# Hybrid attention and retention trunk: a listed first supertile, tables on GpSimd, and outputs loaded two tiles ahead

## The chip, the cores and the metric

The kernel runs on one core of a Trainium2 chip. The time is that of the core on the device, in microseconds (us), from the launch of the program to its end; a profiled execution also gives a span, from the first to the last instruction that the profiler recorded. Engines are named as the profile names them: PE is TensorE, DVE is VectorE, ACT is ScalarE, POOL is GpSimd, SP is SyncE, whose queue issues nearly all DMAs here. Each engine takes its instructions in the order in which they stand in its queue; a waiting instruction holds up all that stand behind it.

## The reference

Two layers and a last RMS norm, on one sequence of 2048 tokens of width 1024:

```
for layer in range(2):
    h    = rms_norm(x, norm_gain[layer])
    proj = h @ w_in[layer]                      # 1024 x 4096: aq ak av ag rq rk rv rg, 512 each
    ya   = chunked attention(aq, ak, av) + relative bias    # 8 heads x 64, own chunk + 8 before
    yr   = retention(rotary(rq), rotary(rk), rv)             # 4 heads x 128, decaying state
    y    = concat(ya * silu(ag), yr * silu(rg))
    x    = x + y @ w_out[layer]                 # 1024 x 1024
out = rms_norm(x, final_gain)
```

The rotary phases come from the positions: cos and sin of position times 64 frequencies. The angles reach 2048 radians, so they are first reduced to (-pi, pi) in several exact steps.

## The kernel before

**Tiles.** The 2048 tokens are 16 tiles of 128, or four supertiles of 512 (n = 0 to 3). The heads are taken in four groups s (two attention heads and one retention head each). For each layer l and each s, the kernel goes through the four supertiles: `dense_T` computes q, k, rq, rk with channels on partitions, `dense_V` computes v, gates and rv with tokens on partitions, and `attention` (which carries `retention` along) works on the supertile whose projections came just before. Every matrix product is made of three float16 products (high with high, high with low, low with high), so one supertile's `dense_T` or `dense_V` is 96 matmuls of 512 columns (L630, L650).

**The normed input.** `norm` makes hT(l, n), the transposed high and low halves of the normed tokens, tile by tile: a sum of squares on ACT (L207), the inverse root on POOL (L210), the product with it on ACT (L231) or DVE (L229), the product with the norm gain, spread to all partitions by a DMA (`gain_load`), on POOL (L233) or DVE, the split on ACT and DVE (L249, L250), and the transposes by DMA (L254, L255) or, for the first four tiles, by PE (`transpose_split`). The four supertiles' hT lie in the pool `hp`, four buffers for each half.

**The tables.** `tables` computes cos and sin of one supertile: 21 short instructions on DVE on 128x256 tiles, two Sin on ACT, and eight DMAs to DRAM (L130 to L133), from where `dense_T` loads them for each s (L559, L560); POOL then turns rq and rk (L595 to L597).

**The order.** PE, ACT, DVE and POOL run in the order in which the Python code emits instructions (`manual_schedule`); the DMAs on SP are ordered by a scheduler. Each generator yields at points about 8 matmuls apart. `run` steps one main generator (dense or output), at each yield also one step of the attention generator, and pulls steps of background work out of the list `bg` (`push(generator, steps)`), spread over the given number of yields (`thirds`). If a table is needed that isn't there, `tab_load` pulls background work until it is. For the first supertile the order is written out by hand (L1005 to L1050), as calls of `go_on` on generators.

**The output stage.** `wout` goes through the 16 tiles. A tile is 48 matmuls (L892) in six steps of eight, two column halves c, each half followed by the residual sum on DVE (L895). Its input is y (written by the attention to DRAM), loaded (`y_load`, L792), measured and scaled by a power of two (`y_scale`, L800 to L811: a sum of squares on ACT for the first six tiles of layer 0 and all of layer 1, else a maximum on DVE, then a product on ACT), split in two float16 rows (`y_split`) and transposed by DMA (`y_turn`). In tile t the step i = 1 splits y of t + 1, i = 2 turns it and loads y of t + 2, i = 5 scales y of t + 2. In layer 0 the sum goes to DRAM (L901) and is normed in place for the next layer (`norm`, one step of it at i = 1, 2, 3, 5, and its transposes at the next tile's i = 0); in layer 1 `final` norms it and stores it. The y tiles, the x tiles (`x_load`, L797) and the weight sections share the four buffers of the pool `w4`.

Of the kernel before, what the change touches and what calls it, by code (L numbers as in the profile page):

```python
# [18 lines left out]
P = 128  # L19
# [8 lines left out]
def hybrid_trunk(ctx: ExitStack, tc: tile.TileContext, x, pos, gain, gcol, w_in, w_out, rel, fgain,  # L28
# [53 lines left out]
    def tables(ns, wks):  # L82

        for n, wk in zip(ns, wks):
            ang, k, r, k2 = (wk[:, i, :] for i in range(4))
            pi = k2.bitcast(I32)
            for hf in range(2):
                o = n * 512 + hf * 256
                sp.dma_start(pi[hf * 64:(hf + 1) * 64, :], pos[None, o:o + 256].to_broadcast([64, 256]))

            def mulsub(dst, kk, c):
                dve.scalar_tensor_tensor(out=dst, in0=kk, scalar=-c, in1=dst, op0=ALU.mult, op1=ALU.add)

            def rnd(dst, src, mul):
                dve.tensor_scalar(dst, src, mul, MAGIC, op0=ALU.mult, op1=ALU.add)
                dve.tensor_scalar(dst, dst, -MAGIC, None, op0=ALU.add)

            dve.tensor_copy(ang, pi)
            dve.tensor_scalar(ang, ang, invf_sb[:, 0:1], None, op0=ALU.mult)
            rnd(k, ang, 1.0 / P1)  # L100
            for c in (PA, PB, PC):
                mulsub(ang, k, c)
            yield
            dve.tensor_scalar(k2, k, -(PD + PE_), None, op0=ALU.mult)
            dve.tensor_tensor(k2, k2, ang, op=ALU.add)
            rnd(k2, k2, 1.0 / TWO_PI)
            mulsub(ang, k2, QA)
            mulsub(ang, k, PD)
            yield
            mulsub(ang, k2, QB)  # L110
            mulsub(ang, k, PE_)
            mulsub(ang, k2, QC)
            yield
            dve.tensor_scalar(ang, ang, PI_CL, -PI_CL, op0=ALU.min, op1=ALU.max)
            dve.tensor_scalar(k, ang, HALF_PI, -TWO_PI, op0=ALU.is_gt, op1=ALU.mult)
            dve.tensor_tensor(k, k, ang, op=ALU.add)
            dve.tensor_scalar(k, k, HALF_PI, PI_CL, op0=ALU.add, op1=ALU.min)
            yield
        for wk in wks:
            ang, k, r, k2 = (wk[:, i, :] for i in range(4))  # L120
            act.activation(r, ang, AF.Sin)
            act.activation(k2, k, AF.Sin)
            dve.tensor_scalar(ang, r, -1.0, None, op0=ALU.mult)
        yield
        for n, wk in zip(ns, wks):
            ang, k, r, k2 = (wk[:, i, :] for i in range(4))
            for hf in range(2):
                sl = slice(hf * 64, hf * 64 + 64)
                cs = slice(hf * 256, hf * 256 + 256)
                sp.dma_start(tab_d[n][0, 0:64, cs], k2[sl, :])  # L130
                sp.dma_start(tab_d[n][0, 64:128, cs], k2[sl, :])
                sp.dma_start(tab_d[n][1, 0:64, cs], ang[sl, :])
                sp.dma_start(tab_d[n][1, 64:128, cs], r[sl, :])  # L133
            tab_done.add(n)
            yield
# [64 lines left out]
    def rms(xt, m, e, nm, junk, on_dve=False):  # L200

        ss = b2.tile([P, 1], F32, tag="ss", name=f"ss{nm}")
        if on_dve:
            dve.tensor_tensor_reduce(out=junk, in0=xt, in1=xt, scale=1.0, scalar=0.0, op0=ALU.mult, op1=ALU.add,
                                     accum_out=ss)
        else:
            act.activation(junk, xt, AF.Square, accum_out=ss)  # L207
        dve.tensor_scalar(ss, ss, m, e, op0=ALU.mult, op1=ALU.add)
        rs = b2.tile([P, 1], F32, tag="rs", name=f"rs{nm}")
        pool.tensor_tensor(rs, ss, mhalf, op=ALU.pow)  # L210
        return rs
# [7 lines left out]
    def norm(l, t, xt, sq_dve=False, mul_dve=False, by_pe=False, rows=None):  # L219
# [5 lines left out]
        rs = rms(xt if sq_dve else xt.rearrange("p (k c) -> p k c", c=P), gains[l].m, gains[l].e, nm,  # L225
                 psS.tile([P, D], F32, tag="S", name=f"pj{nm}") if sq_dve else hh, sq_dve)
# [8 lines left out]
        if by_pe:  # L235
            transpose_split(xt, hh, hl, nm)
            yield
            return
# [5 lines left out]
    def split_rows(xt, nm, rows=None):  # L244
# [4 lines left out]
        act.activation(rows[0], xt, AF.Copy)  # L249
        dve.tensor_tensor(rows[1], xt, rows[0], op=ALU.subtract)  # L250
# [6 lines left out]
    def transpose_split(src, dh, dl, nm):  # L257
        for h in range(2):
            k0, k1 = h * KT // 2, (h + 1) * KT // 2
            pt = psR.tile([P, KT // 2, P], F32, tag="small", name=f"pt{nm}_{h}")  # L260
            for kt in range(k0, k1):
                pe.transpose(pt[:, kt - k0, :], src[:, kt * P:(kt + 1) * P], ident)
            act.activation(dh[:, k0:k1, :], pt, AF.Copy)
            dve.tensor_tensor(dl[:, k0:k1, :], pt, dh[:, k0:k1, :], op=ALU.subtract)
# [108 lines left out]
    def prep_V(l, s, g, quick=False):  # L373
# [16 lines left out]
        def rest(k):  # L390
            for _ in range(0 if quick else k):
                yield
# [793 lines left out]
```

## Time and profile before

| | us |
|---|---|
| median of 3 runs | 2241.95 |
| lowest and highest run | 2240.34 and 2249.49 |
| the profiled execution | 2245.32 |
| its span | 2243.5 |
| PE busy in the span | 2061.8 (92%) |
| DVE, ACT, POOL busy | 1052.2, 1049.1, 813.3 |

The profile is of one execution, which took 3.4 us more than the median; what lies outside its span is 1.8 us. Busy time is the time in which an engine had an instruction under way; PE's matmuls are pipelined, so a matmul's own duration (some 0.38 us) is longer than the step from one to the next (0.22 us).

### The profile page before, as it was taken

The page shows a single profiled execution, that of the slowest core. Times are in us where ns is not written, and L with a number is a line of the kernel's source. Part 1 is how long each engine was busy: PE and PEld are TensorE (multiplying, and loading weights), DVE is VectorE, ACT ScalarE, POOL GpSimd, SP SyncE. Part 2 cuts the span into 40 slices and gives each one's busy share as a digit, 9 for nine tenths or more (in the row PEclk, how much of TensorE's full clock was granted, in tenths as well). Part 3 has the DMA queues.
Part 4 walks back from the last instruction along what each step waited for, and adds up shares of the span by engine and source line. Part 5 has one row for each costly group of instructions (what it writes and reads, how often), then busy time and mean ns, then how long its engine had stood idle before and what let it go on. Part 6 is the DMA issues. An engine that isn't in the chain of part 4 may idle for free.

```text
span 2243.5 us, 37852 instructions
## 1 busy us (share of the span) xinstructions
PE 2061.8 (92%) x13590; PEld 1107.4 (49%) x13590; DVE 1052.2 (47%) x3326; ACT 1049.1 (47%) x1938; POOL 813.3 (36%) x856
## 2 busy tenths in 40 slices
PE   5575999999999999988788999999999999998887
PEld 4233555555555555543333555555555555554333
DVE  5355554445544543456533534454444454445443
ACT  5346454645444544555442545454544454454332
POOL 1444344344443433332223334443454343332100
PEclk9798999999999999999999999999999999999999
DMA  7867555756444644679884445556555455447765
GB/s 212 191 154 166 118 116 123 171 110 133 117 108 103 131 114 90 135 179 235 195 185 127 108 99 111 128 137 146 113 123 118 101 128 121 92 103 170 174 165 145
DMA packets 624541, 308.30 MB, mean 137 GB/s; under 512 B 438080, under 2 KB 580928, under 8 KB 624352
## 3 DMA queue, kind: packets, MB, share of 16 engines
q1 hardware_dynamic: 624352, 305.88, 59.9%
q8 instruction: 107, 1.75, 0.3%
q14 instruction: 82, 0.67, 0.1%
HBM read 123.26 MB, written 41.98 MB: 74 GB/s over the span
## 4 chain that ended last, share of the span: by engine, by line
PE 67%; DMA 7%; ACT 6%; DVE 5%; issue 4%; SPq 2%; POOL 2%; POOLq 0%; ACTq 0%; DVEq 0%
PE dT L630 25%; PE dV L650 25%; PE dO L892 4%; DMA x_d<-xxy 2%; PE S L692 2%; PE S L691 2%; DMA yyy<-y_d 2%; PE o L713 1%; PE o L712 1%; PE o L711 1%; PE r L751 1%; PE r L760 1%; PE r L764 1%; PE r L762 1%; ACT yjy L803 1%
## 5 line engine op out<-in xcount | busy, mean ns | idle before, releaser
L701 POOL TENSOR_TENSOR pq<-sc,pq 128x640 f16<-128x640 f32 (+4 forms) x256 | 320.1, 1250 | 831.9 <-ACT pq L700 423.8
L698 ACT ACTIVATE sc<-sc,mq,cT 128x640 f32<-128x640 f32 (+4 forms) x256 | 218.5, 853 | 646.5 <-DVE mq L697 337.0
L630 PE MATMUL dT<-hTh,whT 128*128 128x512 f16 x1008 | 386.4, 383 | 30.2 <-DMA hTh<-rhn 25.7
L650 PE MATMUL dV<-whV,hTh 128*128 128x512 f16 x1024 | 389.1, 380 | 2.4 <-ACT rot L585 2.4
L650 PE MATMUL dV<-wlV,hTh 128*128 128x512 f16 x1024 | 389.0, 380 | 0.0
L650 PE MATMUL dV<-whV,hTl 128*128 128x512 f16 x1024 | 389.0, 380 | 0.0
L630 PE MATMUL dT<-hTl,whT 128*128 128x512 f16 x1008 | 385.8, 383 | 0.2 <-DMA hTl<-rln 0.2
L630 PE MATMUL dT<-hTh,wlT 128*128 128x512 f16 x1008 | 385.9, 383 | 0.0
L630 PEld LDWEIGHTS <-whT 128*128 128x128 f16 x2016 | 198.0, 99 | 252.1 <-issue 40.2
L650 PEld LDWEIGHTS <-hTh 128*128 128x128 f16 x2048 | 200.2, 98 | 219.3 <-issue 10.6
L695 DVE CUSTOM_DVE_ANT_0 sc<-S,bias 128x640 f32<-128x640 f32 (+4 forms) x256 | 189.1, 739 | 212.5 <-PE S L692 184.2
L892 PE MATMUL dO<-whO,yhy 128*128 128x512 f16 x512 | 197.9, 387 | 30.5 <-DMA yhy<-rhy 17.5
L892 PE MATMUL dO<-whO,yly 128*128 128x512 f16 x512 | 197.6, 386 | 13.1 <-DMA yly<-rly 13.0
L892 PE MATMUL dO<-wlO,yhy 128*128 128x512 f16 x512 | 197.4, 386 | 3.0 <-DVE wlO L312 3.0
L700 ACT ACTIVATE pq<-sc 128x640 f16<-128x640 f32 (+4 forms) x256 | 171.5, 670 | 10.1 <-DMA pT<-pq 2.0
L892 PEld LDWEIGHTS <-yhy 128*128 128x128 f16 x1024 | 99.0, 99 | 155.2 <-DMA yhy<-rhy 26.9
L775 POOL TENSOR_TENSOR rss<-rss,mhalf 128x1 f32<-128x1 f32 x128 | 88.9, 694 | 191.4 <-DVE rss L774 170.0
L691 PE MATMUL S<-k,q 128*128 128x128 f16 (+3 forms) x592 | 143.2, 268 | 9.0 <-DVE mq L695 5.4
L650 PEld LDWEIGHTS <-hTl 128*128 128x128 f16 x1024 | 100.3, 98 | 102.6 <-issue 1.1
L630 PEld LDWEIGHTS <-wlT 128*128 128x128 f16 x1008 | 99.3, 99 | 101.3 <-issue 6.1
L661 DVE SCALAR_TENSOR_TENSOR v<-dV,v 128x128 f16<-128x128 f32 x128 | 37.1, 290 | 216.3 <-ACT rv L660 216.3
L711 PE MATMUL o<-v,pT 128*128 128x65 f16 x1120 | 129.9, 194 | 9.0 <-DMA pT<-pq 9.0
(248 smaller groups left out, 3448.6 us busy)
## 6 DMA issues: line engine op xcount, KB each, us to landing
stV<-in_w_in_dram SPq DMA_DIRECT2D x32, 512.0 KB, 4.5
q<-qq SPq DMA_DIRECT2D x128, 128.0 KB, 2.5
swp<-rot SPq DMA_DIRECT2D x128, 128.0 KB, 2.4
yyy<-y_d SPq DMA_DIRECT2D x32, 512.0 KB, 4.2
stT<-in_w_in_dram SPq DMA_DIRECT2D x28, 512.0 KB, 4.8
k<-kk SPq DMA_DIRECT2D x128, 64.0 KB, 2.0
tabc<-tab SPq DMA_DIRECT2D x32, 256.0 KB, 2.9
tabs<-tab SPq DMA_DIRECT2D x32, 256.0 KB, 3.0
```

The source lines that it names most:

```text
L630: pe.matmul(ps, w_[:, j, kt, :], h_[:, kt, :], start=(m == 0), stop=(m == 23))
L650: pe.matmul(ps, h_[:, kt, a * P:(a + 1) * P], w_[:, kt, :], start=(m == 0), stop=(m == 23))
L661: dve.scalar_tensor_tensor(out=st.v[:, a, :, 65:129], in0=pv_, scalar=2.0 ** -16, in1=vh_, op0=ALU.mult, op1=ALU.subtract)
L691: pe.matmul(o, st.q[:, hx, 0, cs], k_, start=True, stop=False)
L692: pe.matmul(o, st.q[:, hx, 1, cs], k_, start=False, stop=True)
L695: dve.tensor_tensor_reduce(out=v, in0=S[:, 0:w], in1=g.bias[hx][:, 640 - w:640], scale=1.0, scalar=-3.0e38, op0=ALU.add, op1=ALU.max, accu ...
L698: act.activation(v, v, AF.Exp, bias=m[:, 0:1], scale=g.c[:, 0:1])
L700: act.activation(pq[:, 0:w], v, AF.Copy)
L701: pool.tensor_tensor(pq[:, w:2 * w], v, pq[:, 0:w], op=ALU.subtract)
L711: pe.matmul(o[:, 0:65], u.p[:, b, :], v_[:, 0:65], start=(b == 0), stop=False)
L775: pool.tensor_tensor(ss, ss, mhalf, op=ALU.pow)
L892: pe.matmul(ps, h_[:, kt, :], w_[:, kt, :], start=(m == 0), stop=(m == 23))
```

## The change

Four things are changed.

1. **The first supertile.** The hand-written calls become a list of single steps (`do("xsq0 xrs0 gb ...")`): each token tile's square, inverse root, product, transposes and split (`Tok`), each weight section's square, scale and split, the 18 steps `d` of the first `dense_T`, and the steps `t` of the table. The list also holds the weights of the first `dense_V` and the norm of tiles 4 to 7, all products of which DVE makes; their loads are issued at the start, into hT buffers that are still free. Their last steps and the bias tiles stand in `rounds`, one for each yield of the first `dense_V`.
2. **Tables and norm gain.** The table of supertile 0 is computed on POOL, where a multiply-and-add is two instructions, and those of the others on DVE, in 18 steps each; each table is pushed a supertile ahead, woven with the norm of the same supertile. The norm gain of layer 0 is loaded as one row and spread over the partitions by PE (`gain_rows`). The scale of layer 1's gain moves from a background step to the second supertile of s = 1, and the weights of s = 1 are prepared in the last supertile of s = 0 and not from the third one on. The DRAM scratch of the bias is reused between groups.
3. **The output stage.** The scale is a maximum on DVE for every tile; the product with it is no longer a pass of its own but part of the split. In tile t, i = 0 turns y of t + 1 and loads y of t + 2, i = 3 scales and i = 4 splits y of t + 2.
4. **Buffers.** x tiles lie in hT buffers that are free by then (12 of 16 tiles in layer 0, all in layer 1), y tiles from the ninth on in the two buffers `q`.

The core of the diff, cut:

```diff
-    def tables(ns, wks):
+    def tables(n, wk, on, pi=None):
...
+        def mulsub(dst, kk, c):
+            if on is dve:
+                on.scalar_tensor_tensor(out=dst, in0=kk, scalar=-c, in1=dst, op0=ALU.mult, op1=ALU.add)
+            else:
+                on.tensor_scalar(r, kk, -c, None, op0=ALU.mult)
+                on.tensor_tensor(dst, dst, r, op=ALU.add)
...
-        act.activation(rows[0], xt, AF.Copy)
-        dve.tensor_tensor(rows[1], xt, rows[0], op=ALU.subtract)
+        if s_ is None:
+            act.activation(rows[0], xt, AF.Copy)
+            dve.tensor_tensor(rows[1], xt, rows[0], op=ALU.subtract)
+        else:
+            act.activation(rows[0], xt, AF.Copy, scale=s_[:, 0:1])
+            dve.scalar_tensor_tensor(out=rows[1], in0=xt, scalar=s_[:, 0:1], in1=rows[0], op0=ALU.mult, op1=ALU.subtract)
...
-            d = dp.tile([P * RELW], F32, tag=f"toep{l}_{h}", name=f"toep{l}_{h}")
+            d = dp.tile([P * RELW], F32, tag=f"toep{h % 4}", name=f"toep{l}_{h}")
...
     def y_load(l, t):
-        u.y = w4.tile([P, D], F32, tag="w4", name=f"yy{u.nm}")
+        if t < 8:
+            u.y = w4.tile([P, D], F32, tag="w4", name=f"yy{u.nm}")
+        else:
+            u.y = b2.tile([P, D], F32, tag="q", name=f"yy{u.nm}")
...
     def x_load(l, u):
-        u.x = w4.tile([P, D], F32, tag="w4", name=f"xx{u.nm}")
+        if l + 1 == DEPTH or u.t < 12:
+            f = (hT[l, 0] if l + 1 == DEPTH else hT_of(l + 1, NS - 1))[u.t // 2 % 2].rearrange("p k c -> p (k c)").bitcast(F32)
+            u.x = f[:, u.t % 2 * D:(u.t % 2 + 1) * D]
+        else:
+            u.x = w4.tile([P, D], F32, tag="w4", name=f"xx{u.nm}")
...
     def y_scale(l, u, go):
-        if u.t < 6 or l + 1 == DEPTH:
-            junk = b1.tile([P, D], F16, tag=("qq", "tabc")[u.t % 2], name=f"yj{u.nm}")
-            act.activation(junk, u.y, AF.Square, accum_out=m)
-            dve.tensor_scalar(m, m, 2.0 ** -100, None, op0=ALU.max)
-            sy, iy = norm_scale(m, u.nm)
-        else:
-            dve.tensor_reduce(m, u.y, axis=AX.X, op=ALU.max, apply_absolute_value=True)
-            sy, iy = pow2_scale(m, 2.0 ** -80, u.nm)
-        act.activation(u.y, u.y, AF.Copy, scale=sy[:, 0:1])
+        dve.tensor_reduce(m, u.y, axis=AX.X, op=ALU.max, apply_absolute_value=True)
+        u.sy, iy = pow2_scale(m, 2.0 ** -80, u.nm)
...
     def wout(l, go, gc, us, wT=None):
-                if i == 0 and pturn is not None:
-                    next(pturn, None)
+                if i == 0:
+                    if pturn is not None:
+                        next(pturn, None)
+                    if t + 1 < NT:
+                        y_turn(us[t + 1])
+                    if t + 2 < NT:
+                        us.append(y_load(l, t + 2))
...
-                if i == 1 and t + 1 < NT:
-                    y_split(us[t + 1])
-                if i == 2 and t + 1 < NT:
-                    y_turn(us[t + 1])
-                    if t + 2 < NT:
-                        us.append(y_load(l, t + 2))
-                if i == 5 and t + 2 < NT:
+                if i == 3 and t + 2 < NT:
                     y_scale(l, us[t + 2], go)
+                if i == 4 and t + 2 < NT:
+                    y_split(us[t + 2])
...
+    def gain_rows():
+        ps = psS.tile([P, D], F32, tag="S", name="gbp")
+        for h in range(2):
+            pe.matmul(ps[:, h * 512:(h + 1) * 512], one[0:1, :], row[0:1, h * 512:(h + 1) * 512], start=True, stop=True)
+        act.activation(gains[0].b, ps, AF.Copy)
...
+    do("xsq0 xrs0 gb xmul0 Wsq0 xtr0 Wlp0 xsq1 Wsc0 xhi0 t xlo0 Wcv0 xrs1 xsq2 Wcv0 t xsq3 xmul1 d Wsq1 xrs2 xtr1 xrs3 xhi1 "
+       "Wlp1 t xmul2 Wsc1 Wsq2 xtr2 xhi2 t Wlp2 xlo1 Wsc2 Wcv1 r t xlo2 Wcv2 d Wsq3 xmul3 r t d Vsq0 Wlp3 Wcv1 Wcv1 Wsc3 xtr3 "
+       "xhi3 d t Vlp0 Wcv3 xlo3 Vsc0 Vsq1 d t Vcv0 Vlp1 Wcv2 Wcv2 d Vsq2 Vsc1 t d Wcv3 Wcv3 Vcv1 d t Vcv0 d r Vsq3 d t Vcv1 d "
+       "Vlp2 xsq4 d bs t xsq5 xrs4 Vsc2 vu d Vcv2 t d xmul4 xrs5 xsq6 d t Vcv3 Vcv2 vu xhi4 d xmul5 t Vcv3 xsq7 xrs6 d t d "
+       "xlo4 xhi5 xmul6 t")
...
+    t1 = tables(1, xs0[1].rearrange("p (k c) -> p k c", c=256), dve)
+    push(rounds(["xdma4 xlo5 xhi6 t", "xdma5 xlo6 xrs7 xmul7 t", "xdma6 xhi7 xlo7 t u", "xdma7 t u", "u u bt", "u u", "u u",
+                 "u u", "u u", "u u bt", "u u", "u u u"]), 12)
...
-                    if n == 1:
-                        push(tabs[0], 6)
-                    if 0 < n and n + 1 < NS:
-                        push(norms_from_input(range(4 * n + 4, 4 * n + 8)), 21)
-                    if n == 1:
-                        push(tabs[1], 6)
-                    if n == 2:
-                        push(tabs[2], 6)
-                        push(gains_rest(), 2)
-                if n == min(2 if (l, s) == (0, 0) else 1, NS - 1):
+                if (l, s) == (0, 0) and 0 < n < NS - 1:
+                    tb = tables(n + 1, xs0[n + 1].rearrange("p (k c) -> p k c", c=256), dve)
+                    push(weave(norms_from_input(range(4 * n + 4, 4 * n + 8)), tb), 21 + TAB_STEPS)
...
+                if n == (NS - 1 if (l, s) == (0, 0) else 1):
```

408 lines of the change are left out of this document (231 added, 177 removed).

## The prediction

> **What bounds the kernel now.** I read the page first, then the busy time by stage, then the longest waits of PE.
>
> ```profile
> span 2243.5 us, 37852 instructions
> PE 2061.8 (92%) x13590; PEld 1107.4 (49%) x13590; DVE 1052.2 (47%) x3326; ACT 1049.1 (47%) x1938; POOL 813.3 (36%) x856
> ```
>
> PE is the bound, and 181.7 us of the span is PE standing still. Where, is told by PE's busy time in stretches that follow the stages (columns: stretch, its length, busy us and instructions of PE, weight loads, DVE, ACT, POOL; granted clock; DMA share; GB/s).
>
> ```profile
> 0.00:59.00 59.00, 33.70 (x298) 25.16 (x299) 31.76 (x88) 28.33 (x43) 9.98 (x31) 0.94 0.72 217
> 59.00:106.00 47.00, 21.31 (x99) 9.44 (x97) 15.53 (x36) 20.10 (x33) 24.34 (x20) 0.78 0.82 180
> 106.00:250.00 144.00, 103.62 (x614) 53.74 (x614) 82.07 (x239) 75.27 (x130) 60.64 (x54) 0.89 0.72 155
> 250.00:944.00 694.00, 690.50 (x4892) 386.76 (x4890) 323.39 (x1135) 335.86 (x667) 288.45 (x305) 1.00 0.55 120
> 1028.00:1192.00 164.00, 126.73 (x558) 53.42 (x559) 82.03 (x168) 74.77 (x100) 34.97 (x29) 0.98 0.84 199
> 2088.00:2237.00 149.00, 131.47 (x611) 55.50 (x609) 57.49 (x130) 50.92 (x74) 9.81 (x15) 1.00 0.64 166
> ```
>
> The long middle (250 to 944) idles for 3.5 us in 694: nothing is to be had there. The idle time lies in the first 250 us (25.3 + 25.7 + 40.4 = 91.4 us) and in the two output stages (37.3 and 17.5 us in the stretches shown). Those are the places the change touches.
>
> **1. The first supertile and the gap behind it.** These rows of the timeline give the first matmul of `dense_V`, the next stage's first matmul and what POOL did meanwhile.
>
> ```profile
> 59.17 0.38 PE L650 MATMUL dV<-whV,hTh 128*128 128x512 f16 x1
> 105.75 0.58 PE L630 MATMUL dT<-hTh,whT 128*128 128x512 f16 x1 [25.69 <-DMA hTh<-rhn]
> 81.75 1.26 POOL L595 TENSOR_TENSOR rot<-rot,tabc 128x512 f32<-128x512 f32 x1 [5.74 <-DMA tabc<-tab]
> 87.93 2.34 POOL L233 TENSOR_TENSOR hTh<-hTh,gb 128x1024 f32<-128x1024 f32 x1
> ```
>
> PE waits 25.7 us for the norm of tiles 4 to 7, whose gain product (L233) stands in POOL's queue behind the turn (L595), which waits for the table. In the changed list those products are on DVE, and the four tiles are normed ahead of or in the first `dense_V`. What is late next? I bound the start of `dense_V` by its queues, in the order of the built program.
>
> ```profile
> 11.60 1.06 ACT L207 ACTIVATE hTh<-xa 128x1024 f16<-128x1024 f32 x1 [1.55 <-DMA xa<-in_x_dram]
> 51.16 2.19 ACT L309 ACTIVATE whV<-stV,sV 128x1024 f16<-128x1024 f32 x2 [1.27 <-DVE iV L159]
> 22.08 0.19 POOL L193 TENSOR_TENSOR cT<-cT,iT 128x1 f32<-128x1 f32 x1
> 86.06 1.91 POOL L524 TENSOR_SCALAR bias<-bias,ciT 128x640 f32<-128x640 f32 x1
> 7.55 0.55 POOL L210 TENSOR_TENSOR rsn<-ssn,mhalf 128x1 f32<-128x1 f32 x1 [6.13 <-DVE ssn L208]
> 21.76 0.24 POOL L191 TENSOR_SCALAR cT<-iT 128x1 f32<-128x1 f32 x1
> 53.10 1.18 POOL L191 TENSOR_SCALAR raV<-gqkV 128x1 f32<-128x1 f32 x1 [0.48 <-DVE gqkV L431]
> 52.93 2.48 DVE L312 SCALAR_TENSOR_TENSOR wlV<-stV,sV,whV 128x1024 f16<-128x1024 f32 x2
> ```
>
> DVE, up to the last split of the V weights: 6 products, 8 weight splits and 4 token splits of about 1.25 us (half of the 2.48 for two; 22.5), some 60 short ones of 0.16 (L146 below) to 0.2 (11), two evacuations and the bias copies (2.5): 36 us from about 5.5, so not before 41.5. ACT has 29 passes of about 1.1 us there, so it ends no later than DVE. POOL stands ahead of that last split too: tile 5's inverse root (L210) has 25 table instructions before it. None is in the trace at 128x256. On the straight line through 0.24 (128x1) and 1.91 (128x640), a TENSOR_SCALAR takes 0.9 us, and through 0.19 and 1.26 (128x512), a TENSOR_TENSOR 0.73: 16 x 0.9 + 9 x 0.73 + 5 x 0.55 + 11 x 0.21, with the copy as one more 0.7, is 26.7 us. They start when the positions have landed, five 512 KB loads after the second x tile's place (11.6): I take 15. So POOL lets DVE through at 42 at the earliest. From the other side, raV took 1.18 where its like took 0.24, and it ran beside a weight split of DVE (52.93): one waits for the other. Eleven such DVE instructions of 1.2 us in that time add up to 13 us: 55. With two more DVE instructions behind it `dense_V` starts between 44 and 59; I take 52, nearer the upper end, since DVE is busy for most of this time.
>
> The Trainium skill has a rule that speaks against the move: SBUF — State Buffer, section "Who interferes with whom", says that a VectorE instruction with two SBUF inputs and a GpSimd instruction that reads SBUF exclude each other, and that whichever comes second waits for the whole of the other. The pair at 53 us agrees with it; by the rule at every encounter the start would be the 59 of my range.
>
> `dense_V` itself is 96 matmuls; the following row gives 16,
>
> ```profile
> 249.27 3.45 PE dV L650 x16
> ```
>
> and the next one is the nearest to a DMA of the table or the turn (last column: us from issue to landing).
>
> ```profile
> swp<-rot SPq DMA_DIRECT2D x128, 128.0 KB, 2.4
> ```
>
> So 20.7 us: it ends at 73. Tile 7, the last, is normed by then: from tile 5's root another 6 us of POOL to its own, 3.5 on DVE and ACT, and an estimated 6 for two transposes by DMA (2.4 for a transfer, twice, and their issue) is 15 us, against 2.6 + 20.7: 8 us of cover. The turn of rq and rk is tighter. Behind tile 5's root stand 4.5 us of table, an estimated 10 for its stores and its load (2.4 each, several in a row on one queue), twice 3.8 for the turns (three of 1.26), 2.4 for rk's swap and 2 to 4 for a bias product: about 28, and PE asks for it after 27. I allow 2 us. The next `dense_T` then runs from 75 instead of 105.75: **31 us won** (from 20, with the upper end and a late turn, to 40).
>
> **2. The other supertiles of s = 0** (106 to 250, idle 40.4 us at a clock of 0.89). The largest piece:
>
> ```profile
> 218.50 0.19 PE L302 MATMUL msg<-mbg,ones 128*128 128x1 bf16 x1 [15.86 <-DVE mbg L296]
> 209.21 0.28 DVE L98 CAST xb<-xb 128x256 f32<-128x256 int32 x1
> ```
>
> PE waits for a one-column matmul behind supertile 3's whole table, which `tab_load` pulls into DVE's queue in one go (from 209.21). With the tables a supertile ahead and one step at a time this wait of 15.9 us goes. Of the other 24.5 us, with the clock of 0.89, I take 11 off, since one table less falls on n = 1 and the norms are spread thinner, and put 5 back: the weights of s = 1 are now prepared in one supertile instead of two, and each brings a one-column matmul (L302) that waits for DVE. The 11 and the 5 are choices, not sums, so the range is wide. **22 us won**, from 8 (if only half the large wait goes) to 32.
>
> **3. Output stage of layer 0.** A part of the chain of work that ended last, in order (start, duration, what):
>
> ```profile
> 1130.79 5.15 DMA x_d<-xxy
> 1136.05 1.16 ACT xxy L231
> 1137.27 2.36 POOL xxy L233
> 1139.65 1.07 ACT rhn L249
> 1140.74 1.23 DVE rln L250
> 1141.97 1.14 DVE ymy L807
> 1143.13 0.16 DVE ymy L146
> ...
> 1143.86 0.67 DVE xxy L895
> 1144.55 5.20 DMA x_d<-xxy
> ```
>
> This is a ring, once per tile, 13.76 us, where 48 matmuls take 10.35: the store of x must land before the norm overwrites it in place, the norm's split stands on DVE ahead of the maximum of a later y, and that ahead of the residual sum, which the next store waits for. The change does not cut it; it takes the maximum and its four small ones (1141.97 to 1143.86, 1.9 us) from behind the split to ahead of it, where they lie under POOL's 2.36. The new scaled split (ACT 1.1, DVE 1.25) lies there too. The ring is then 11.9 us plus some 0.2, eleven tiles, at most 20 us. Against that, the DMA rings:
>
> ```profile
> q1 hardware_dynamic: 18543, 10.01, 86.3%
> ```
>
> That is from 1110 to 1165, four tiles: 0.863 x 55 / 4 = 11.9 us of DMA per tile, and the change moves the same bytes. Where transfers crowd, the store's 5.15 may grow. I take 12.5 per tile, so 14 us. In the first five tiles, with attention woven in, y is turned two steps earlier (i = 0, not 2); I count 1. **15 us won**, from 0 (DMA keeps the pace) to 28.
>
> **4. Output stage of layer 1.** The same view there:
>
> ```profile
> 2133.45 5.35 PE dO L892 x24
> 2138.80 4.32 issue
> 2143.12 1.16 ACT yjy L803 x2
> ...
> 2145.80 5.36 PE dO L892 x24
> ```
>
> 12.35 us per tile: y is loaded only behind the turn before it, its landing ends the 4.32, and its scale on ACT, DVE and again ACT comes before its own turn. In the built program SP's queue holds each y load a tile earlier, and buffers are free for it; ACT loses two of its passes per tile and DVE gains 1.2 + 0.1, of 5.4 before in 12.35. The next bound is PE's 10.35; I take 10.6 for eleven tiles (19), and 1 for the first five: **20 us won**, from 10 to 25.
>
> **Sum.** 31 + 22 + 15 + 20 = 88 us. The profiled execution's 2245.3 would become 2157; the median lies 3.4 lower: **2154**. Everything between 250 and 944 and in layer 1's attention is the same work in the same order and counts nothing; its cover, PE at 99%, doesn't depend on the change.
>
> **The rivals.**
> - *The DMA rings keep the pace of layer 0's output stage*: for it speaks the 86%, against it that y and x loads now spread over the tile. 15 us less: 2169.
> - *GpSimd sets the start*: every encounter with DVE costs in full, the turn comes late by another 8 us. 15 us less: 2169. The 1.18 of raV speaks for it; that most POOL rows are within 2% of each other, against.
> - *The later supertiles still stall*: the norm's POOL product stays in its queue between attention's, and the denser weights take the rest; only the large wait is won, with a new one of 10 us in n = 3. 2170.
> - *All ends fall well*: start at 44, ring at 11.9, PE's floor in layer 1: 88 + 30, so 2124.
> - *Slower*: one table instruction on POOL has a form that no row shows (two operations at once, a comparison). The root (L210) took 0.55 for one column where a sum took 0.19: 0.36 us more per column, which at 256 columns is 92 us, in the queue ahead of tile 5's root and so of PE. 2154 + 92 = 2246. It decides from 88 us, 0.34 per column, in one instruction, or 3.5 us in each of the 25. The product and sum rows speak against it; the comparison is open.
> - *The change doesn't do what it says*: if SP's queue held a y load behind the turn of the tile before, part 4 would win nothing and part 3's ring would close through the load. The built order speaks against it. 2185 to 2195.
>
> **How the numbers follow.** The forecast (2135 to 2175 with its own errors, which takes in the first three rivals' times) has 0.52; DMA pace alone with something else 0.12, GpSimd 0.10, later stalls 0.10; all falls well 0.08; slower 0.04; loads not ahead 0.04. From 2112 (the well-fallen case with 12 more) to 2200 (two of the first three rivals and the loads) no more than 2 in 10 is left out. A measurement of this kernel can tell about 0.5%, 11 us, from no change: faster has all but the slow case and a little beside it, 0.94; same 0.02; slower 0.04.
>
> **What would show it.** In the profile after: the wait of 25.7 us ahead of n = 1's first matmul gone, and that matmul at 70 to 80 us; if it comes at 85 or later, POOL's rows between 15 and 55 us show whether 128x256 takes more than 0.9. No wait over 5 us for L302 near 200 us. The stores of x 12 to 13 us apart in layer 0, with the maximum ahead of the norm's split. Layer 1's tiles 10.4 to 11 us apart. I would be wrong if PE's new first wait is the turn (rq, rk), if SP's transposes queue behind x loads that wait for their buffer, or if the DMA share in the output stage reads 0.95 and the stores take 7 us.

## The result, and the profile after

The changed kernel takes **2188.68 us** (median of 4 runs, 2186.89 to 2189.29), the kernel before 2241.98 in the runs beside them: a ratio of **0.9755** (95% interval 0.9732 to 0.9777), 53 us less. The forecast was 2154, 88 us less. The profiled execution took 2189.29 us, its span is 2187.5.

The busy times of the page, and the busy times in stretches that follow the stages (length, busy us of PE, weight loads, DVE, ACT, POOL, granted clock, DMA share, GB/s). The stretches are cut at the first matmuls of the stages and of tiles 5 and 10 of the output.

```profile
PE 2063.1 (94%) x13594; PEld 1114.0 (51%) x13594; DVE 1094.7 (50%) x3330; ACT 990.2 (45%) x1861; POOL 837.4 (38%) x882
```

```profile
0.00:49.75 49.75, 37.15 (x302) 26.89 (x303) 31.94 (x86) 34.98 (x54) 34.81 (x54) 1.00 0.91 269
49.75:85.16 35.41, 24.74 (x97) 10.00 (x96) 23.67 (x32) 11.05 (x20) 21.77 (x24) 0.90 0.79 173
85.16:288.03 202.87, 166.86 (x1061) 89.52 (x1062) 110.54 (x312) 103.91 (x191) 86.49 (x77) 0.92 0.65 150
919.91:1000.50 80.59, 69.21 (x468) 36.75 (x469) 50.78 (x129) 33.97 (x53) 25.47 (x21) 0.96 0.84 196
1000.50:1076.40 75.90, 58.96 (x245) 24.65 (x244) 44.17 (x95) 33.17 (x51) 15.72 (x16) 0.91 0.80 205
1076.40:1153.77 77.37, 65.06 (x291) 28.37 (x290) 39.58 (x62) 29.23 (x35) 19.63 (x13) 0.98 0.66 155
1991.66:2066.30 74.64, 67.34 (x468) 36.23 (x469) 47.30 (x130) 27.90 (x48) 18.40 (x18) 0.98 0.75 185
2066.30:2180.40 114.10, 114.10 (x529) 51.55 (x527) 61.05 (x112) 24.61 (x34) 7.31 (x12) 1.00 0.61 163
```

The kernel before, cut at the same matmuls of its own timeline; of its rows, these are part 2, tiles 5 to 9 of part 3 and the rest of part 4:

```profile
105.75:311.24 205.49, 165.11 (x1063) 88.57 (x1064) 109.79 (x337) 106.31 (x190) 85.35 (x77) 0.93 0.66 143
1028.40:1094.90 66.50, 53.05 (x244) 23.02 (x244) 42.92 (x92) 36.93 (x54) 15.14 (x16) 1.00 0.87 215
2101.90:2236.40 134.50, 119.36 (x528) 49.76 (x528) 49.94 (x106) 44.69 (x64) 7.30 (x12) 1.00 0.61 163
```

The lengths of all parts beside each other, with the forecast of each:

| part | before, us | after, us | difference | forecast |
|---|---|---|---|---|
| 1: to the first `dense_T` of n = 1 | 105.75 | 85.16 | -20.6 | -31 |
| 2: n = 1 to 3 of s = 0 | 205.49 | 202.87 | -2.6 | -22 |
| 3: output stage of layer 0, tiles 0 to 4 / 5 to 9 / 10 to the end | 84.2 / 66.5 / 85.5 | 80.6 / 75.9 / 77.4 | -3.6 / +9.4 / -8.1 | -15 in all |
| 4: output stage of layer 1, tiles 0 to 4 / the rest | 81.5 / 134.5 | 74.6 / 114.1 | -6.9 / -20.4 | -20 in all |

The rest of the span's 56.0 us, 3.2, lies in the dense stages between. So part 4 gave more than forecast, part 1 two thirds, and parts 2 and 3 nearly nothing: each won what was named and lost it again in a new wait.

**Where the time of parts 1 and 2 went.** PE's five longest waits between 50 and 230 us in the changed kernel's timeline (start, duration, instruction, in brackets the idle time before it and what ended it):

```profile
54.98 0.47 PE L695 MATMUL dV<-wlV,hTh 128*128 128x512 f16 x1 [4.84 <-DVE wlV L353]
71.06 0.38 PE L695 MATMUL dV<-whV,hTh 128*128 128x512 f16 x1 [4.09 <-DVE gt L708]
128.50 0.80 PE L805 MATMUL r<-rv,dT 128*128 128x128 f32 x2 [5.25 <-DVE dT L802]
153.33 0.59 PE L675 MATMUL dT<-hTh,whT 128*128 128x512 f16 x1 [8.21 <-ACT rv L705]
228.56 0.59 PE L675 MATMUL dT<-hTh,whT 128*128 128x512 f16 x1 [8.68 <-DVE v L706]
```

The 25.7 us ahead of n = 1 and the 15.9 us of L302 are gone; the last two rows, ahead of the first matmuls of n = 2 and n = 3, are new. What led to the wait at 153 is read in two queues of the changed kernel's timeline, SP's (issues) and ACT's.

```profile
140.78 0.48 SPq L132 DMA_DIRECT2D tab<-xb  x1
...
145.14 0.59 SPq L135 DMA_DIRECT2D tab<-xb  x1
...
146.98 1.25 SPq L748 DMA_TRANSPOSE pT<-pq  x1
```

```profile
151.67 0.63 ACT L745 ACTIVATE pq<-sc 128x512 f16<-128x512 f32 x1 [5.07 <-DMA pT<-pq]
152.21 0.26 ACT L703 ACTIVATE v<-dV 128x128 f16<-128x128 f32 x1
```

SP issues the eight stores of supertile 2's table without a break, 5 us. The transpose of attention's weights (`pT`), whose input POOL finished at 143.44 (142.28 + 1.16), stands behind them and is issued at 146.98; it has landed when ACT goes on at 151.67; only then does ACT evacuate `dense_V` (L703), for which PE waits. The same pattern ends the wait at 228, and the first table's stores (55.0 to 61.5) stand in the same way ahead of the transposes of tiles 4 to 7, which leads to the 4.09 us at 71.

**Where the time of part 3 went.** The chain of waits of the changed kernel through one of the tiles 5 to 9, in order (start, duration, what); short pieces between are left out:

```profile
1040.10 3.38 DMA x_d<-hTl
...
1044.64 1.33 ACT whT L329 x4
...
1045.99 1.19 DVE m1T L331
...
1047.37 1.14 DVE ymy L853
...
1049.15 1.16 ACT rhy L251
...
1051.54 1.22 DVE rln L249
1052.75 0.66 DVE hTl L941
```

SP's queue in the same kernel at the end of that chain:

```profile
1053.35 1.26 SPq L257 DMA_TRANSPOSE yly<-rly  x1
1054.70 1.29 SPq L257 DMA_TRANSPOSE hTl<-rln  x1
1056.08 0.53 SPq L947 DMA_DIRECT2D x_d<-hTl  x1
```

From store to store it is 15.98 us. The store lands in 3.4 us, faster than the 5.15 before. But the split of y (ACT 1.16, then DVE 1.2 until 1051.54) stands between the maximum and the norm's split, and SP has y's and the norm's transposes to issue before the store: the sum is ready at 1053.41, the store goes at 1056.08, 2.7 us later.

### The profile page after: what moved, and what is told of

Its sections match the earlier page's. It is cut to its first block, busy times and chain, and to the rows that moved or that the text cites. A ratio compares the mean times of both kernels' runs of the same rounds, so it can differ in the third digit from the quotient of the medians.

```text
span 2187.5 us, 37773 instructions
## 1 busy us (share of the span) xinstructions
PE 2063.1 (94%) x13594; PEld 1114.0 (51%) x13594; DVE 1094.7 (50%) x3330; ACT 990.2 (45%) x1861; POOL 837.4 (38%) x882
## 4 chain that ended last, share of the span: by engine, by line
PE 70%; DVE 9%; ACT 7%; DMA 5%; issue 4%; POOL 3%; SPq 2%; ACTq 0%; POOLq 0%; DVEq 0%
PE dT L675 25%; PE dV L695 25%; PE dO L938 6%; PE S L736 2%; PE S L737 2%; ACT sc L743 2%; DVE sc L740 1%; PE o L756 1%; PE o L757 1%; PE o L758 1%; PE r L805 1%; PE r L796 1%; PE r L809 1%; PE r L807 1%; DMA pT<-pq 1%
## 5 line engine op out<-in xcount | busy, mean ns | idle before, releaser
L938 PEld LDWEIGHTS <-yhy 128*128 128x128 f16 x1024 | 101.3, 99 | 137.2 <-issue 28.3
```

The lines of the kernel that those rows point to most:

```text
L938: pe.matmul(ps, h_[:, kt, :], w_[:, kt, :], start=(m == 0), stop=(m == 23))
```

## The experiments

They ran in three groups (e1 to e4, e5 to e8, e9 to e12), each beside runs of the kernel before (2241.99, 2245.99 and 2239.36 us), so times of different groups are compared by their ratio to it: 0.001 is 2.2 us. The changed kernel's ratio is 0.9755. Below, the pitch is the time from one tile of the output stage to the next, and its floor is PE's own time for 48 matmuls, 10.35 us.

**e1_tab_act** takes the stores of three tables off SP's queue:

```diff
+        q = sp if n == 0 else act
...
-            sp.dma_start(tab_d[n][0, 0:64, cs], k2[sl, :])
-            sp.dma_start(tab_d[n][0, 64:128, cs], k2[sl, :])
+            q.dma_start(tab_d[n][0, 0:64, cs], k2[sl, :])
+            q.dma_start(tab_d[n][0, 64:128, cs], k2[sl, :])
+            if n:
+                yield
...
```

> The changed kernel, but the eight table stores of supertiles 1 to 3 are issued by ACT, two to a step, and not by SP eight in a row. Theory, SP's queue: the transposes of attention's weights (pT) stand behind the eight stores (5 us of issue each time), ACT's next pass waits for pT and holds the evacuation of dense_V, so the first matmul of n = 2 and of n = 3 waits 8.2 and 8.7 us. Then these two waits fall to 3 to 5 us each and the time to 2178 to 2184. Rival, the transfers: the same bytes crowd the DMA rings whoever issues them; the waits stay within 1 us and the time within 2186 to 2191.

Measured: 2180.38 us, 0.9724 (0.9709 to 0.9738), 7 us less than the changed kernel by the ratios (8.3 by the medians). The two waits became

```profile
152.98 0.38 PE L680 MATMUL dT<-hTh,whT 128*128 128x512 f16 x1 [1.04 <-DMA hTh<-rhn]
```

```profile
220.78 0.58 PE L680 MATMUL dT<-hTh,whT 128*128 128x512 f16 x1 [2.21 <-ACT sc L748]
```

and n = 1 to 3 takes 195.4 us in place of 202.9 (86.10 to 281.5). With the same bytes, issued elsewhere and two stores to a step, most of the two waits is gone: it was SP's queue, not the transfers. Not all of it is won: a matmul of `dense_T` at 96.20 now waits 4.32 us and one of `dense_V` at 143.56 3.67, where the changed kernel has 0.26 each; the first stands behind a pass of ACT that came late because of ACT's own stores (last section).

**e2_mul_dve** takes POOL's 2.35 us products out of the norm of tiles 8 to 15:

```diff
-                next(nx[t - 2])
...
-                nx[t - 1] = norm(0, t - 1, xt[t - 1])
+                nx[t - 1] = norm(0, t - 1, xt[t - 1], True)
```

> The changed kernel, but the norm of tiles 8 to 15 of layer 0 makes its product with the gain in one DVE instruction of 1.27 us and no longer with 1.14 us on ACT and 2.35 us on POOL. Theory, DVE and POOL shut each other out: eight POOL products of 2.35 us hold short DVE instructions that stand in PE's way (a 128x1 product took 1.96 us in place of 0.16, a 128x256 step 2.56 in place of 0.42), so 4 to 8 us go in the stretch 106 to 250, time 2180 to 2185. Rival, queue length alone: DVE has eight more instructions of 1.27 us in front of attention's, and the stretch gets longer or stays; 2188 to 2194.

Measured: 2189.26 us, 0.9759 (0.9743 to 0.9775): no difference, as the rival had it. The theory isn't empty, though. In the changed kernel the wait of 5.25 us for L802 stands behind a table instruction of DVE that ran beside one of POOL's products (124.34 to 127.11) and took six times its 0.42:

```profile
124.84 2.56 DVE L94 SCALAR_TENSOR_TENSOR xb<-xb 128x256 f32<-128x256 f32 x1
```

With the products on DVE that wait is down to

```profile
127.50 0.49 PE L805 MATMUL r<-rv,dT 128*128 128x128 f32 x2 [1.26 <-DVE dT L802]
```

and the second of its kind falls from 3.97 to 1.81 us. But DVE's longer queue brings others (1.41 and 2.38 us ahead of matmuls of `dense_V` in n = 1), and the waits ahead of n = 2 and 3 stay (8.48 and 9.04 us in place of 8.21 and 8.68), since SP's queue ends them. What is won in one place is lost in the next.

**e3_split_late** moves the split of y behind the sum and its store:

```diff
-                if i == 4 and t + 2 < NT:
-                    y_split(us[t + 2])
...
             if l + 1 < DEPTH:
                 sp.dma_start(x_d[t], u.x)
+            if t + 2 < NT:
+                y_split(us[t + 2])
+            if l + 1 < DEPTH:
                 pturn = pnorm
```

> The changed kernel, but in the output stage y of t + 2 is split behind the residual sum of tile t (end of i = 5) and no longer ahead of it (i = 4). Theory, the ring: in tiles 5 to 9 of layer 0 the ring of 15.85 us runs through the maximum, the split on ACT and DVE (2.4 us) and SP's two transposes of y, which stand ahead of the store of x (2.5 us); the split and the transposes go behind the store, the pitch of these tiles falls from 15.8 to 11.5 to 13.5 us, and the time to 2168 to 2180. Rival, weights of layer 1: the ring is set by ACT's weight squares and DVE's maximum behind POOL's product, and the split lies beside them; the pitch stays above 15 and the time within 2185 to 2190. Layer 1's pitch stays at 10.36 by both.

Measured: 2168.45 us, 0.9672 (0.9657 to 0.9686), **18.6 us less** than the changed kernel by the ratios (20.2 by the medians). Its output stage of layer 0, cut as above (tiles 0 to 4, 5 to 9, the rest):

```profile
918.90:994.70 75.80, 68.05 (x468) 35.62 (x469) 50.12 (x132) 35.12 (x54) 26.48 (x22) 0.98 0.91 209
994.70:1058.40 63.70, 55.96 (x245) 23.96 (x246) 43.81 (x92) 32.20 (x49) 16.50 (x16) 0.95 1.00 247
1058.40:1135.90 77.50, 65.18 (x291) 28.05 (x290) 33.79 (x63) 29.49 (x35) 17.79 (x13) 0.98 0.66 151
```

Tiles 5 to 9 take 63.7 us, 12.7 each, in place of 75.9, and the whole stage 217.0 in place of 233.9. Another 3 us come from the first five tiles of layer 1's stage (71.5 us in place of 74.6). The DMA share in tiles 5 to 9 now reads 1.00 at 247 GB/s (0.80 and 205 in the changed kernel), and 12.7 is near the 12.5 that the prediction gave for DMA's pace. That DMA sets the pace isn't shown, though. In the chain of waits there the store lands in 3.3 us,

```profile
1012.70 3.34 DMA x_d<-hTh
```

and from it the chain goes on as before through ACT's weight squares, m1T (a one-column sum), the maximum, the norm's split and the sum, behind which the next store is issued at 1024.61, 11.9 us after the one before; from there the chain turns to a transpose of y (4.45 us).

**e4_out_old** puts the old output stage into the changed kernel, in `wout`

```diff
-                if i == 3 and t + 2 < NT:
-                    y_scale(l, us[t + 2], go)
-                if i == 4 and t + 2 < NT:
-                    y_split(us[t + 2])
+                if i == 1 and t + 1 < NT:
+                    y_split(us[t + 1])
+                if i == 2 and t + 1 < NT:
+                    y_turn(us[t + 1])
+                    if t + 2 < NT:
+                        us.append(y_load(l, t + 2))
+                if i == 5 and t + 2 < NT:
+                    y_scale(l, us[t + 2], go)
...
```

and in the same way `y_load`, `x_load`, `y_scale`, `y_split` and `wout_first`.

> The changed kernel with the whole output stage of the kernel before (loads, scale, split and turn in the old steps, x and y tiles in the four old buffers). Theory, the stages are independent: layer 0's output stage takes 236 us in place of 234 and layer 1's 223 in place of 196, time 2215 to 2220. Rival, the output stages were helped by the earlier parts of the change (weights and tables due at other times): the loss is under 20 us, time below 2209.

Measured: 2220.72 us, 0.9900 (0.9885 to 0.9914), 32 us more. Layer 0's stage takes 233.6 us, as in the changed kernel (233.9), layer 1's 81.7 + 133.5, as before:

```profile
919.80:1153.40 233.60, 193.71 (x1002) 88.14 (x1003) 126.42 (x283) 115.44 (x161) 61.55 (x49) 0.95 0.83 199
2074.30:2207.80 133.50, 118.78 (x526) 49.69 (x526) 50.15 (x107) 44.70 (x64) 7.31 (x12) 1.00 0.59 164
```

So on balance the whole gain of the new output stage is in layer 1, and the stages are independent of the earlier parts of the change.

**e5_tab0_act** is e1 with the first table's stores on ACT too (the diff is against e1):

```diff
-        q = sp if n == 0 else act
+        q = act
...
-            if n:
-                yield
+            yield
```

> As e1_tab_act, and the eight stores of supertile 0's table too are issued by ACT, two to a step. Theory, SP's queue: the transposes of tiles 4 to 7 stood on SP behind those stores (55 to 61.5 us), ACT's and DVE's splits behind the transposes, and the evacuation of the first dense_V behind the splits, which is the wait of 4.06 us at 71 and part of the next; without them the first dense_V takes 29 to 32 us in place of 35.7, and the time falls by 3 to 7 us below 2180.4: 2173 to 2177. Rival, the table itself: the turn of rq and rk waits for the table either way, and the wait moves to the first matmuls of n = 1's end; 2178 to 2183.

Measured: 2181.91 us, 0.9710 (0.9694 to 0.9727), not told apart from e1_tab_act: by the ratios 3 us less, with intervals that overlap, so the total doesn't decide between the two expectations. The trace speaks for the rival. The first `dense_V` fell to 28.4 us (50.4 to 78.8), as expected, but the gain was lost at once. PE's next wait is

```profile
87.78 0.79 PE L800 MATMUL r<-rot,rot 128*128 128x128 f32 x2 [5.29 <-POOL rot L640]
```

the turn of rq and rk, which waits for the table, whose pairs of stores now go one step after the other. Behind the transposes the table is next.

**e6_pass** makes y's scale a pass of its own again:

```diff
-        u.sy, iy = pow2_scale(m, 2.0 ** -80, u.nm)
+        sy, iy = pow2_scale(m, 2.0 ** -80, u.nm)
+        act.activation(u.y, u.y, AF.Copy, scale=sy[:, 0:1])
...
-        u.rows = split_rows(u.y, u.nm, None, u.sy)
+        u.rows = split_rows(u.y, u.nm)
```

> The changed kernel, but y's scale is a pass of its own on ACT (1.15 us) ahead of an unscaled split, as before; loads, steps and buffers stay new. Theory, loads: layer 1 gained because y lies there two tiles ahead, so its pitch stays at 10.4 and the stage at 196 us; layer 0's ring takes 1.2 us more in tiles 5 to 9, and the time is 2192 to 2200. Rival, passes: ACT's two saved passes made the gain; layer 1's pitch goes to 11 to 12.4 and the time to 2200 to 2215.

Measured: 2195.29 us, 0.9781 (0.9767 to 0.9796), some 6 us more by the ratios. Tiles 6 to 8 of layer 0 take 16.8 to 17.0 us in place of 15.7 to 15.9, one pass more in the ring; layer 1 stays at PE's pace:

```profile
2080.00:2186.00 106.00, 105.95 (x491) 47.84 (x489) 55.94 (x105) 32.05 (x40) 6.75 (x11) 1.00 0.60 165
```

**e7_steps_old** keeps the new forms and buffers but takes `wout_first` and `wout` of the kernel before, with their steps: e4's edit of these two, without the other functions.

> The changed kernel with the old steps of the output stage (y of t + 1 split at i = 1 and turned at i = 2, y of t + 2 loaded at i = 2 and scaled at i = 5) but the new scaled split, the maximum on DVE for every tile and the new buffers. Theory, steps: layer 1's pitch comes back to 11.5 to 12.4 us, the stage to 212 to 222 us, and layer 0's stage to 225 to 236; time 2203 to 2218. Rival, buffers and the merged pass: the load starts early because buffers are free, whatever the step; layer 1's pitch stays under 11, time 2180 to 2195.

Measured: 2186.86 us, 0.9735 (0.9720 to 0.9749), no difference from the changed kernel. My theory fell where it mattered: layer 1 stays at PE's pace with the old steps. Layer 0's stage takes 230.8 us; there the old steps, which split y behind the sum, are no worse than the new ones.

```profile
2060.00:2173.00 113.00, 112.92 (x524) 51.22 (x525) 61.23 (x109) 23.76 (x34) 7.29 (x12) 1.00 0.63 167
```

**e10_buf_old** keeps steps and forms but puts all x and y tiles into `w4`:

```diff
-        if t < 8:
-            u.y = w4.tile([P, D], F32, tag="w4", name=f"yy{u.nm}")
-        else:
-            u.y = b2.tile([P, D], F32, tag="q", name=f"yy{u.nm}")
+        u.y = w4.tile([P, D], F32, tag="w4", name=f"yy{u.nm}")
```

(and the same for x).

> The changed kernel with the x and y tiles of the output stage in the four old buffers; steps, scaled split and maximum stay new. Theory, buffers: the loads can't be issued until a tile is free, layer 1's pitch goes back from 10.36 to 11.5 to 12.4 us and the time to 2202 to 2218. Rival, the measure: what made layer 1 faster is the maximum on DVE in place of the sum of squares on ACT, and the old buffers do; pitch under 10.8, time 2186 to 2195.

Measured: 2200.76 us, 0.9823 (0.9806 to 0.9841), some 15 us more, but all of it in layer 0, whose stage takes 248.1 us; layer 1 is again at PE's pace. So the pitch is the rival's, and neither expectation had the loss in layer 0.

```profile
919.70:1167.80 248.10, 200.46 (x1002) 91.33 (x1003) 124.07 (x286) 96.56 (x138) 60.78 (x49) 0.92 0.76 183
2072.00:2192.00 120.00, 119.50 (x567) 54.37 (x566) 66.27 (x127) 26.05 (x36) 8.39 (x14) 1.00 0.70 188
```

e4, e6, e7 and e10 together: among these runs layer 1's old pitch of 12.3 us comes back only where everything of the new stage is undone. With the old pass, or the old steps, or the old buffers alone it stays at 10.36. The old loop (load, sum of squares, scale, split, turn, next load) was 2 us over PE's floor, and none of these three edits is needed by itself to get down to it. The fourth, the maximum on DVE in place of the sum of squares on ACT, was undone only in e4, together with the rest: whether it does the work alone, or any of several cuts would, stays open.

**e8_both** is e5_tab0_act and e3_split_late in one.

> e5_tab0_act and e3_split_late in one. Theory, separate places: the gains add, 2188.7 less 20.2 and less what e5 gains (8.3 or more): 2153 to 2161. Rival, a shared limit (SP's queue or the clock, which follows PE's rests): under three quarters of the sum, above 2163.

Measured: 2163.88 us, 0.9630 (0.9614 to 0.9647). The ratios of e3 and of e1 and e5 add up to 0.963 to 0.964: separate places, and no shared limit shows. In us, 2163.88 lies just above the rival's bound of 2163, but the kernel before was 4 us slower in this group; by the ratio it is 2159, in the theory's range.

**e9_three** has e3's split, and SP itself issues fewer stores:

```diff
...
-        for hf in range(2):
...
-            sp.dma_start(tab_d[n][1, 64:128, cs], r[sl, :])
+        for i, src in enumerate((k2, ang, r)):
+            sp.dma_start(tab_d[n][i], src)
...
-            sp.dma_start(st.tabc, tab_d[n][0])
-            sp.dma_start(st.tabs, tab_d[n][1])
+            for b_, w_, i in ((st.tabc, 0, 0), (st.tabc, 64, 0), (st.tabs, 0, 1), (st.tabs, 64, 2)):
+                sp.dma_start(b_[w_:w_ + 64, :].rearrange("p (h j) -> p h j", h=2), tab_d[n][i].rearrange("(h c) j -> c h j", h=2))
```

> As e3_split_late, and each table is stored by three DMAs of SP (cosine, minus sine, sine, 128 x 256 each) in place of eight, and loaded by four in place of two. Theory, SP's queue: five issues of some 0.6 us fewer stand ahead of the transposes of tiles 4 to 7 and of attention's pT in n = 1 and 2, and no other engine is made to wait; the first dense_V takes 28 to 32 us, the waits ahead of n = 2 and n = 3 fall from 8 to under 5 us each, time 2153 to 2162. Rival, latency: what counts is the way of the table through DRAM and the turn behind it, and two more loads make up for it; 2165 to 2172.

Measured: 2159.80 us, 0.9640 (0.9623 to 0.9657), some 7 us below e3 by the ratios, with intervals that touch. The first `dense_V` takes 28.3 us:

```profile
49.60:77.91 28.31, 22.89 (x97) 9.68 (x96) 20.26 (x32) 11.07 (x20) 16.40 (x21) 0.94 0.80 174
```

The waits ahead of n = 2 and n = 3 fell only to 5.95 and 6.07 us, and the wait of 5.25 us for L802 grew to 6.46: n = 1 to 3 as a whole takes 203.4 us, as in the changed kernel. So the part of the theory on the first `dense_V` holds, that on n = 2 and 3 hardly does at five issues fewer.

**e11_three_mul** is e9_three with e2's edit.

> As e9_three, and the norm's product of tiles 8 to 15 on DVE as in e2_mul_dve. Theory, DVE and POOL shut each other out: with SP's queue clear, the waits that are left in n = 1 and 2 end on DVE, and they go with POOL's products: 3 to 6 us below e9_three. Rival: DVE's length in these supertiles is what is left, and the product of 1.27 us adds to it: within 2 us of e9_three, or slower.

Measured: 2158.34 us, 0.9634 (0.9614 to 0.9653), no difference from e9_three. In the trace it is as in e2: the waits for L802 fall from 6.46 and 3.97 us to 1.25 and 1.81, and waits of 1.4 to 2.8 us for DVE come in. So with SP's queue short too, giving POOL's products to DVE gains nothing that shows in the total; what DVE's waiting for them costs apart from DVE's longer queue, these runs don't tell.

**e12_tab0_dve** is e9_three with the first table on DVE:

```diff
-    t0 = tables(0, xs0[0].rearrange("p (k c) -> p k c", c=256), pool, pi0)
+    t0 = tables(0, xs0[0].rearrange("p (k c) -> p k c", c=256), dve, pi0)
```

> As e9_three, but the table of supertile 0 is computed on DVE, 21 instructions of 0.28 to 0.45 us, and not on POOL. Theory, POOL sets the start: the splits of the V weights and the roots no longer wait for POOL's table, the first dense_V starts at 46 to 49 us and has no wait of 4 us at its second split; 3 to 6 us below e9_three. Rival, DVE sets it: 7 us more stand in DVE's queue ahead of the last split, the first dense_V starts or stalls 3 to 8 us later; 3 to 8 us above e9_three.

Measured: **2154.82 us**, 0.9618 (0.9597 to 0.9638), the fastest of all. Its interval overlaps that of e9_three, so in the total the difference isn't settled. In the trace `dense_V` starts no earlier (50.27 against 49.60; expected were 46 to 49) but takes 24.0 us in place of 28.3, at the full clock:

```profile
50.27:74.27 24.00, 21.21 (x98) 9.27 (x96) 18.33 (x30) 11.05 (x20) 11.68 (x14) 1.00 0.96 190
```

and its wait for the last weight split is 2.01 us in place of 4.84. So the table on GpSimd, one of the things that the change is named for, shows no gain here, and in this profile costs 4 us. The 7 us that the table adds to DVE's queue moved the start by 0.7 us, so the 3 to 8 us of the rival aren't there.

## Why the prediction was right and wrong

The direction and the outer range (2112 to 2200) held; the likeliest range (2135 to 2175) didn't. The 35 us between 2154 and 2189 come from three steps: parts 1 to 3 fell short by 10, 19 and 13 us. Part 4 gave 7 us and the dense stages between 3 us more than forecast; the other 3 are the difference between medians and profiled executions.

**Part 1, right to the start of `dense_V`, wrong behind it.** It starts at 49.75 (forecast 52, 44 to 59). The nearness is in part luck: the forecast let `dense_V` start behind the last split of its weights, which ended at 54.92. The first matmul didn't need that split; the second did, and waited 4.84 us for it. A table instruction on POOL takes what the line gave where nothing hinders it, 0.85 and 0.72 us, forecast 0.9 and 0.73; beside DVE's instructions some took more (1.94 us for L123 at 52.59).

```profile
23.47 0.85 POOL L96 TENSOR_SCALAR xa<-xa 128x256 f32<-128x256 f32 x1
24.40 0.72 POOL L97 TENSOR_TENSOR xa<-xa 128x256 f32<-128x256 f32 x1
```

The step that failed is "`dense_V` itself is 96 matmuls", 20.7 us with 8 us of cover. It took 35.4, of which 10.7 are waits (4.84 of them for the split just named) and 4 the clock of 0.90. The eight stores of the table were counted for the turn, but not for the transposes of tiles 4 to 7 that stand behind them in SP's queue (from 61.5 us). That used up the cover. e5 and e9 take 7 us of the stage back by shortening that queue, e12 another 4 by taking the table from POOL.

**Part 2, the wait named went, the next one wasn't asked for.** The wait of 15.9 us for L302 is gone, as the step said. But to spread a table over 18 steps doesn't spread its stores: they are one step, eight issues, 5 us of SP, ahead of pT each time. 8.2 + 8.7 us came back that way, and 5.3 and 4.0 in waits for L802. e1 shows it: n = 1 to 3 is 7.5 us shorter. The rival "the later supertiles still stall" was the right one, in the main by another mechanism than it named. POOL's product is behind the waits for L802 (e2), but the two longest are SP's queue, and taking the product away gains nothing in the total.

**Part 3, the failed sentence is "The new scaled split (ACT 1.1, DVE 1.25) lies there too."** It doesn't lie under POOL's product but in the ring, in the tiles that carry layer 1's weights (5 to 9). There the maximum itself starts only at 1047.28, as POOL's product ends: ahead of it stands m1T, a sum of one column, which waits for ACT's weight squares until 1045.97 and then took 1.18 us, to the end of the product, where the products of one column at L763 have a median of 0.16.

```profile
1044.82 2.34 POOL L235 TENSOR_TENSOR hTl<-hTl,gb 128x1024 f32<-128x1024 f32 x1 [2.41 <-ACT hTl L233]
```

```profile
1045.99 1.18 DVE L331 TENSOR_TENSOR m1T<-m1T 128x1 f32<-128x1 f32 x1 [3.02 <-ACT whT L329]
```

So maximum, split of y and norm's split follow each other behind the product, and four transposes stand ahead of the store on SP. In the tiles without weights (10 to 15) the first matmuls follow each other in 10.4 to 14.6 us, 12 on average, near the forecast (before 13.8). The forecast 12.5 was reached in tiles 5 to 9 too as soon as the split moved (e3, 12.7): its position cost 17 us of stage. That number was right; that DMA's pace is the reason for it, as the prediction had it, isn't shown (e3).

**Part 4, the next bound right, size too small.** Pitch 10.36, PE's own, in place of my 10.6; tiles 0 to 4 gave 7 us where I counted 1. Of the reasons that I gave, the early load and the saved scale pass on ACT are not needed, each taken back alone (e6, e7, e10); the saved sum of squares was not tried alone, so which of them made the gain stays open.

**The GpSimd rival** had its place right (the start, 4 us in e12's trace) and its size and the late turn wrong: in the changed kernel the turn is not what PE waits for first; it becomes so in e5, once the transposes are early.

## What to carry to other kernels

When work is woven into steps, weave its DMA issues too: a queue engine that issues for everybody is a resource with a time per instruction (0.6 us for a store, 1.3 for a transpose here), and eight stores in one step are a wait of 5 us for whoever is next. When a pass is moved in a loop that closes through a store, list what stands between the last producer and that store on every queue; a split that nobody needs for another 10 us belongs behind it. And when several cuts bring a chain down to the floor of the bound engine, undo them one at a time before crediting one: here three of four could be taken back singly without loss in layer 1.

## What the runs showed of the hardware

**DVE waits for POOL to the end, even for one column.** In the changed kernel's trace:

```profile
139.97 2.37 POOL L235 TENSOR_TENSOR xin<-xin,gb 128x1024 f32<-128x1024 f32 x1 [0.18 <-ACT xin L233]
```

```profile
140.19 0.16 DVE L762 RECIPROCAL rl<-o 128x1 f32<-128x1 f32 x1
140.38 1.96 DVE L763 TENSOR_TENSOR rl<-rl,kaV 128x1 f32<-128x1 f32 x1
```

Both end at 142.34. The instruction with two inputs in SBUF is held (median 0.159 us over all 256 of its kind, 1.96 here); the one before it, with one input, isn't. That is what the Trainium skill says in SBUF — State Buffer, section "Who interferes with whom": a second SBUF input goes through the read port that DVE shares with GpSimd, and whoever comes second waits for the whole instruction. The trace agrees to 0.02 us. The prediction priced the rule at the start of the first `dense_V`, 59 us if every encounter cost in full; it came at 49.75, and the split that the forecast had ahead of it at 54.92. For the norm's products, the waits of PE behind them shrink in e2 and e11, but the total doesn't.

**A DMA issued by ACT held ACT.** In e8_both ACT issued two pairs of a table's stores at once and the third pair 5 us later, and its next pass came only behind that, 9.17 us after the one before:

```profile
83.80 0.61 ACTq L137 DMA_DIRECT2D tab<-xa  x1
89.65 0.45 ACTq L133 DMA_DIRECT2D tab<-xa  x1
```

```profile
91.11 0.28 ACT L707 ACTIVATE v<-dV 128x128 f16<-128x128 f32 x1 [9.17 <-DMA tab<-xa]
```

The third pair sends the other half of the first pair's tile, so its data was ready when that went out at 81.98. What held it for 5.2 us (84.41 to 89.65) wasn't tried; SP was at that time issuing seven DMAs of the bias, from 81.23 to 92.85. In e1_tab_act the same pass of ACT comes 3.95 us after the one before it, with six stores issued between. Such holds may be why e9_three, which shortens SP's list, does as well as moving the list to another engine.
